# Moving the scratch writes of turned blocks from SyncE's queue to GpSimd's, and reading two kinds of them back one unit later

## The chip, the core and the metric

The kernel runs on one core of one Trainium2 chip. The metric is the device time of one execution in microseconds. The kernel before took 1476.31 us (median of 3 runs, 1476.15 to 1476.97). The execution that the profiler recorded took 1478.79 us, of which 1477.1 us lie between the first and the last instruction (the span); all stretches and waits below are of that execution.

## What is computed

One layer of a hybrid decoder for 256 tokens of width 2048, in float32, with its weights read once from HBM:

```
h = x + hybrid_mixer(rmsnorm(x))          # in-projection, SSD heads and gated short convolutions, out-projection
h = h + memory_cross_attention(rmsnorm(h), rmsnorm(mem))
h = h + (silu(h2 @ w_gate) * (h2 @ w_up)) @ w_down      # h2 = rmsnorm(h)
return rmsnorm(h)

# hybrid_mixer
proj = h @ w_in                            # 2048 -> 11296 columns
z, xbc, dt, sc_u, sc_b, sc_c = split(proj)
xbc = silu(causal_conv(xbc));  y = ssd(xs, dt, a, B, C) + xs * d_skip
y_ssd = grouped_rmsnorm(y * silu(z));  y_sc = grouped_rmsnorm(sc_b * causal_conv(sc_c * sc_u))
return concat(y_ssd, y_sc) @ w_out
```

## The kernel before

**Weights.** All weight matrices stream through the core in one fixed order (`stream_plan`, L138), as tiles of 128x1024 float32 (512 KB), each loaded by one DMA of SyncE's queue (L214) into one of six buffers `r`. Each tile is split in two: ScalarE rounds it to `h` (L254) and VectorE takes the rest, `l = r - h` (L255); the buffer of `r` is free when VectorE is done with it. TensorE multiplies in fp32r: activation parts times `h` (L328, L329) and times `l` (L332), 12 matmuls of 128x512 for a tile, into PSUM tiles `a` of 128 tokens by 512 columns.

**Units.** The program is written out unit by unit (`unit`, L401). A unit holds two weight tiles as a rule (one in the value, output and first gate tiles); it issues loads up to six tiles ahead, splits its tiles and the next two, emits the matmuls, and after the first part of the unit advances every running follow-up by one step. The follow-ups (`group_post`, `u_post`, `to_features`, `heads` and those that they call) are generators: a `yield` puts what follows it into the next unit. TensorE and SyncE run their instructions in exactly this order; on ScalarE, VectorE and GpSimd a scheduler sets the order at build time.

**Pair units.** Some units take a pair of tiles with 21 matmuls in place of 24 (`seven_mm`, L647: L657, L658, L660). They need sums of the two tiles first (`pair_sums`, L223): four VectorE additions (L229 to L232), three ScalarE roundings (L236) and three VectorE subtractions (L237), besides the split of both tiles. The sums take a buffer `b`, of which there are two.

**Turned blocks.** The result of a column group has tokens on the partitions, and what comes next needs features there. So the result is scaled (L359), transposed in 32x32 blocks by VectorE into a buffer `b` (`turn_blocks`, L343, L347), written to a scratch `w` in DRAM (`put`, L362, the DMA of L365, 512 KB) and read back rearranged into a buffer `f` (`get`, L368, the DMA of L372, 512 KB). This is done 42 times: for 22 column groups of the in-projection (`group_post`, L595), 11 gate blocks of the FFN (`u_post`, L304), 7 blocks of the residual (`to_features`, L1002; an eighth goes by TensorE) and for keys and queries (`heads`, L1133). In `group_post` and `u_post` the write is issued one unit after the transposition, the read-back one unit after the write, and the work on `f` one unit after that. All 42 writes and all 42 reads are issued by SyncE, in the same queue as the weight loads. What reads `f` first is, on the in-projection's groups, the copy of a convolution (L740), a silu (L848), or a product (L872, L889); in the FFN it is the split of the gate block (L1319, L1320).

**GpSimd** has little to do before: the setup, a reciprocal square root at a time (L308, L903, L1400) and, once for each of the four SSD groups, six `affine_select` masks (L714, L718 in `decay`, L696) on tiles that a DMA of ScalarE's queue has brought (`s<-acsT`).

Of the kernel before, what the change touches and what calls it, by code (L numbers as in the profile page):

```python
# [150 lines left out]
def trunk(tc, wst, vecs, xp, xtp, mp, mtp, wdt_in, nfin, outp):  # L151
    nc = tc.nc
# [8 lines left out]
    with ExitStack() as ctx:  # L161
# [18 lines left out]
        def nm(s):  # L180
            cnt[0] += 1
            return f"{s}{cnt[0]}"

        def slot(shape=(128, 512), dt=F32):
            return sp.tile(list(shape), dt, tag="s", name=nm("s"))
# [157 lines left out]
        def turn_blocks(src):  # L343

            t = bp.tile([128, 1024], F32, tag="b", name=nm("b"))
            for tb in range(2):
                nc.vector.transpose(t[:, tb * 512:tb * 512 + 512], src[tb])  # L347
            return t

        def scaled(accs, r, adds=None):  # L350

            o = [slot() for _ in range(2)]
            for tb in range(2):
                src = accs[tb]
                if adds is not None:
                    c, op = adds[tb]
                    tt(o[tb], src, c, op)
                    src = o[tb]
                act(o[tb], src, AF.Identity, scale=r[:, tb:tb + 1])  # L359
            return o  # L360

        def put(t):  # L362

            w = drp.tile([2, 128, 512], F32, tag="w", name=nm("w"), bufs=2)
            nc.sync.dma_start(w.rearrange("t p k -> p t k"), t.rearrange("p (t k) -> p t k", t=2))  # L365
            return w

        def get(w):  # L368


            d = fp.tile([128, 1024], F32, tag="f", name=nm("f"))
            nc.sync.dma_start(d.rearrange("p (x c) -> p x c", x=8),  # L372
                              w.rearrange("t (a i) (b c) -> (i b) (t a) c", a=4, b=4))
            return d.rearrange("p (x f j) -> p f x j", x=8, f=4)
# [220 lines left out]
        def group_post(n, accs):  # L595
            t = turn_blocks(scaled(accs, scales["x"], in_corr.pop(n, None)))
            yield
            w = put(t)
            yield
            d = get(w)  # L600
            yield
            if isinstance(groups[n], tuple):
                yield from posts[groups[n][0]](groups[n][1], d)
                return
            for f, (kind, _, j) in enumerate(groups[n]):
                p = posts[kind](j, d[:, f])
                if next(p, 0) is None:
                    procs.append(p)
                if f < 3 and not (kind == "xs" and j % 2 == 0):
                    yield  # L610
# [52 lines left out]
        def first_unit(kt):  # L663

            def part(key, o, ps):
                tok_mm(ps, key, side_blocks(xn, kt - o), (0, 1), kt == 0, kt == KT - 1, (o,))

            def loads():
                if kt + 2 < KT:
                    prep_x(kt + 2)  # L670

            if kt == 0:
                unit([([("a0",)], lambda: (part(("a0",), 0, first[0]), loads())),
                      ([("b0",)], lambda: part(("b0",), 0, first[1]))])
            else:
                key = ("ab", kt)
                unit([([key], lambda: (part(key, 0, first[0]), part(key, 1, first[1]), loads()))],
                     [group_post(0, first[0]), after(2, group_post(1, first[1]))] if kt == KT - 1 else None)
# [269 lines left out]
        for parts in in_units():  # L948
            keys = [k for part in parts for k in part]
            for _, n, c in keys:  # L950
                if n not in iaccs:
                    iaccs[n] = [acc(), acc()]
                    if len(parts[0]) == 2 and n % 2:
                        shared["in", n - 1] = [msc() for _ in range(4)]
                if c == 1:
                    for one in [] if isinstance(groups[n], tuple) else groups[n]:
                        if one[0] == "B" and one[2] > 0:
                            procs.append(decay(one[2]))
            _, n, c = keys[-1]
            quiet = len(parts[0]) == 2  # L960
            post = [group_post(k[1], iaccs[k[1]]) for k in keys if k[2] == KT // 2 - 1]
            unit([(list(part), lambda part=part: in_mm(part)) for part in parts], None, not quiet)
            for q in post:
                next(q)
                procs.append(q)
            if len(parts[0]) == 2:
                in_post(n - 1, shared["in", n - 1])
# [30 lines left out]
        def wait(k):  # L998
            for _ in range(k):
                yield  # L1000
# [132 lines left out]
        def heads(accs, r, dst, steps=(1, 1, 1)):  # L1133

            t = turn_blocks(scaled(accs, r))
            yield from wait(steps[0])
            w = put(t)
            yield from wait(steps[1])
            d = get(w)
            yield from wait(steps[2])  # L1140
            with tc.high_priority():
                for i in range(2):
                    a = slot()
                    o = a.rearrange("p (f x j) -> p f x j", f=2, x=8)
                    if i:
                        nc.vector.tensor_copy(o, d[:, 2:4])
                    else:
                        nc.scalar.copy(o, d[:, 0:2])
                    dst.append(a)

        KTs, Vs, qs = [], [], []
        for m, tiles in (("k", mh), ("q", h1g)):
            accs = [acc(), acc()]
            last = KT // 2 - 2
            for c in range(0, last, 2):
                unit([([(m, k)], lambda k=k: tok_mm(accs, (m, k), side_blocks(tiles, 2 * k), (0, 1), k == 0, False))
                      for k in (c, c + 1)])

            def last_mm(tb):
                for k in (last, last + 1):  # L1160
                    tok_mm(accs, (m, k), side_blocks(tiles, 2 * k), (tb,), False, k == last + 1)

            keys = [(m, last), (m, last + 1)]
            unit([(keys, lambda: last_mm(0)), (keys, lambda: last_mm(1))],
                 heads(accs, scales["mem"], KTs) if m == "k" else heads(accs, xa["sc"], qs, (2, 1, 0)))
# [121 lines left out]
        def whole(m, n, tb, ps):  # L1287

            if n not in SEVEN:
                return ps  # L1290
            c, op = corr[n][m, tb]
            tt(c, ps, c, op)  # L1292
            return c
# [10 lines left out]
        def u_post(n, accs):  # L1304
            while n not in gate:
                yield
            for tb in range(2):
                s = gate[n][tb]
                stt(s, whole("u", n, tb, accs[tb]), ff["r"][:, tb:tb + 1], s, ALU.mult, ALU.mult)  # L1309
            t = turn_blocks(gate[n])  # L1310
            yield
            w = put(t)
            yield
            d = get(w)
            yield
            for i in range(2):
                hi, lo = slot(dt=F32R), slot(dt=F32R)
                hv, lv = [a.rearrange("p (f x j) -> p f x j", f=2, x=8) for a in (hi, lo)]
                nc.scalar.copy(hv, d[:, 2 * i:2 * i + 2])  # L1319
                tt(lv, d[:, 2 * i:2 * i + 2], hv.bitcast(F32), ALU.subtract)  # L1320
                gs[2 * n + i] = hi, lo
# [15 lines left out]
        for i, parts in enumerate(ffn_units()):  # L1337
            if i == len(ffn_units()) - 3:
                token_sums(("d", 0, 0), [gs[0]])
            if i == 8:  # L1340
                for c in range(3):
                    token_sums(c, [(h2g[2 * c + k][:, 0:T], h2g[2 * c + k][:, T:]) for k in range(2)], c == 2)
            post = []
            for part in parts:
                m, n, c = part[0]
                for k in part:
                    if k[2] == 0:
                        faccs[k[:2]] = [acc(), acc()]
                if len(part) == 2:
                    if c == 0:  # L1350
                        shared[n] = [msc() for _ in range(4)]
                    elif c == SEVEN[n] - 1:
                        post.append(p_post(n, shared[n]))
                elif c == KT // 2 - 1:
                    post.append((g_post if m == "g" else u_post)(n, faccs[m, n]))
            unit([(list(part), lambda part=part: part_mm(part)) for part in parts], post or None)
# [274 lines left out]
```

## Time and profile before

| quantity | value |
|---|---|
| median of 3 runs | 1476.31 us |
| the profiled execution | 1478.79 us |
| its span | 1477.1 us |
| TensorE busy in the span | 1461.6 us (99%) |
| VectorE, ScalarE, GpSimd busy | 1279.7, 885.4, 38.5 us |
| mean granted TensorE clock | 0.999 |
| bytes moved by DMA | 350.91 MB, 238 GB/s in the mean |

The stages of the span: the first 16 tiles to about 50 us, the rest of the in-projection to about 600 us, out-projection and attention to about 770 us, the FFN's gate and up projections to about 1240 us, its down projection to 1468 us. In the views, a row of the timeline gives start and length in us, engine, line, operation, output <- input, and in brackets the idle time before it and what ended it. SPq is SyncE's DMA queue; its waits hold up what stands behind them in that queue. In the views of before, line numbers are those of the code above; the changed code has one more from L600 on and two more from L1314 on.

### The profile page before, as it was taken

The page shows a single profiled execution, that of the slowest core. Times are in us where ns is not written, and L with a number is a line of the kernel's source. Part 1 is how long each engine was busy: PE and PEld are TensorE (multiplying, and loading weights), DVE is VectorE, ACT ScalarE, POOL GpSimd, SP SyncE. Part 2 cuts the span into 40 slices and gives each one's busy share as a digit, 9 for nine tenths or more (in the row PEclk, how much of TensorE's full clock was granted, in tenths as well). Part 3 has the DMA queues.
Part 4 walks back from the last instruction along what each step waited for, and adds up shares of the span by engine and source line. Part 5 has one row for each costly group of instructions (what it writes and reads, how often), then busy time and mean ns, then how long its engine had stood idle before and what let it go on. Part 6 is the DMA issues. An engine that isn't in the chain of part 4 may idle for free.

```text
span 1477.1 us, 18980 instructions
## 1 busy us (share of the span) xinstructions
PE 1461.6 (99%) x6568; PEld 1203.6 (81%) x6568; DVE 1279.7 (87%) x1865; ACT 885.4 (60%) x1263; POOL 38.5 (3%) x46
## 2 busy tenths in 40 slices
PE   9999999999999999999999999999999999999997
PEld 7778888888887888888888888888888887888886
DVE  6678899989999775897578999999999998979995
ACT  7576665967765544665466665556655554655663
POOL 0012000101000000000000000000000000000000
PEclk9999999999999999999999999999999999999999
DMA  9777758769677575777648766656676667765553
GB/s 362 248 251 263 259 202 296 253 215 313 224 258 261 193 262 188 253 270 279 224 171 295 265 220 224 220 215 225 228 247 247 220 228 229 268 228 190 195 201 112
DMA packets 151520, 350.91 MB, mean 238 GB/s; under 512 B 11616, under 2 KB 63232, under 8 KB 151424
## 3 DMA queue, kind: packets, MB, share of 16 engines
q1 hardware_dynamic: 142368, 342.83, 66.1%
q10 hardware_dynamic: 9056, 6.87, 1.6%
q8 instruction: 51, 0.84, 0.2%
q14 instruction: 45, 0.37, 0.1%
HBM read 323.40 MB, written 26.26 MB: 237 GB/s over the span
## 4 chain that ended last, share of the span: by engine, by line
PE 67%; DVE 1%; issue 0%; ACT 0%; DVEq 0%; POOLq 0%; POOL 0%
PE a L328 17%; PE a L329 17%; PE a L332 17%; PE m L660 3%; PE m L657 3%; PE m L658 3%; PE a L658 2%; PE a L657 2%; PE a L660 2%; PE m L1207 0%; PE m L1176 0%; PE m L804 0%; PE m L1195 0%; DVE g L1309 0%; DVE f L1292 0%
## 5 line engine op out<-in xcount | busy, mean ns | idle before, releaser
L254 ACT CAST h<-r 128x1024 fp32r<-128x1024 f32 (+1 forms) x539 | 562.3, 1047 | 401.7 <-PE a L329 190.0
L255 DVE TENSOR_TENSOR l<-r,h 128x1024 fp32r<-128x1024 f32 (+1 forms) x539 | 649.5, 1216 | 120.3 <-ACT h L254 114.9
L328 PE MATMUL a<-h,s 128*128 128x512 f32 x1671 | 655.0, 392 | 1.1 <-ACT h L254 1.1
L329 PE MATMUL a<-h,s 128*128 128x512 f32 x1671 | 651.0, 390 | 0.0
L332 PE MATMUL a<-l,s 128*128 128x512 f32 x1671 | 450.0, 390 | 0.0
L328 PEld LDWEIGHTS a<-h,s 128*128 128x128 f32 x1671 | 313.9, 188 | 68.2 <-ACT h L254 2.2
L332 PEld LDWEIGHTS a<-l,s 128*128 128x128 f32 x1671 | 313.7, 188 | 65.6 <-DVE l L255 0.4
L329 PEld LDWEIGHTS a<-h,s 128*128 128x128 f32 x1671 | 314.1, 188 | 64.0
L236 ACT CAST s<-b 128x512 fp32r<-128x512 f32 x110 | 67.6, 618 | 71.3 <-DVE b L229 65.4
L237 DVE TENSOR_TENSOR s<-b,s 128x512 fp32r<-128x512 f32 x110 | 75.6, 687 | 0.8 <-ACT s L236 0.7
L347 DVE STREAM_TRANSPOSE b<-s 128x512 f32<-128x512 f32 x62 | 40.9, 691 | 7.2 <-ACT s L359 7.2
L229 DVE TENSOR_TENSOR b<-r,r 128x512 f32<-128x512 f32 x55 | 37.7, 686 | 10.3 <-DMA r<-in_w_dram 9.8
L230 DVE TENSOR_TENSOR r<-r 128x512 f32<-128x512 f32 x55 | 37.9, 689 | 0.8
L232 DVE TENSOR_TENSOR r<-b,r 128x512 f32<-128x512 f32 x55 | 37.7, 686 | 0.1
L237 DVE TENSOR_TENSOR s<-r,s 128x512 fp32r<-128x512 f32 x55 | 37.7, 685 | 0.0
L236 ACT CAST s<-r 128x512 fp32r<-128x512 f32 x55 | 33.9, 617 | 6.2 <-DVE r L232 5.1
L231 DVE TENSOR_TENSOR b<-b,r 128x512 f32<-128x512 f32 x55 | 37.7, 685 | 0.0
L745 DVE SCALAR_TENSOR_TENSOR t<-t,vec,t 128x255 f32<-128x255 f32 (+2 forms) x72 | 32.4, 479 | 2.8 <-ACT t L742 2.3
L657 PE MATMUL m<-s,t 128*128 128x512 f32 x76 | 29.6, 389 | 0.0
L660 PE MATMUL m<-s,t 128*128 128x512 f32 x76 | 29.6, 389 | 0.0
L658 PE MATMUL m<-s,t 128*128 128x512 f32 x76 | 29.6, 389 | 0.0
L660 PE MATMUL m<-l,s 128*128 128x512 f32 x72 | 28.1, 391 | 1.2 <-DVE l L255 1.2
(248 smaller groups left out, 1395.4 us busy)
## 6 DMA issues: line engine op xcount, KB each, us to landing
r<-in_w_dram SPq DMA_DIRECT2D x535, 512.0 KB, 4.8
w<-b SPq DMA_DIRECT2D x42, 512.0 KB, 3.3
f<-w SPq DMA_DIRECT2D x42, 512.0 KB, 4.8
s<-acsT ACTq DMA_DIRECT2D x24, 256.0 KB, 5.5
s<-in_xt_dram SPq DMA_DIRECT2D x16, 256.0 KB, 6.9
s<-in_mt_dram SPq DMA_DIRECT2D x8, 256.0 KB, 5.2
s<-in_m_dram SPq DMA_DIRECT2D x8, 256.0 KB, 5.8
parked<-s SPq DMA_DIRECT2D x8, 256.0 KB, 8.1
```

The costliest lines, as they stand in the source:

```text
L230: tt(u[:, a], u[:, a], u[:, b], ALU.add)
L236: nc.scalar.copy(h, x)
L237: tt(l, x, h.bitcast(F32), ALU.subtract)
L254: nc.scalar.copy(h[:, c], r[:, c])
L255: tt(l[:, c], r[:, c], h[:, c].bitcast(F32), ALU.subtract)
L328: mm(ps[tb], ah, h[:, w], start=first and i == ks[0], stop=False)
L329: mm(ps[tb], al, h[:, w], start=False, stop=False)
L332: mm(ps[tb], blocks(i, tb)[0], l[:, i * 512:i * 512 + 512], start=False, stop=stop and i == ks[-1])
L347: nc.vector.transpose(t[:, tb * 512:tb * 512 + 512], src[tb])
L657: mm(ps, ah, bh, start=any(ps is q for q in start), stop=False)
L658: mm(ps, al, bh, start=False, stop=False)
L660: mm(ps, ah, bl, start=False, stop=any(ps is q for q in stop))
```

## The change

`put` takes the queue that issues its DMA, GpSimd's unless another is given. `heads` gives SyncE's, so its two writes stay where they were; the other 40 writes move. All 42 reads stay on SyncE. `group_post` and `u_post` get a second `yield` between write and read-back, so that in 33 cases the read, and what the program emits behind it, come one unit later.

```diff
-        def put(t):
+        def put(t, queue=nc.gpsimd):
 
             w = drp.tile([2, 128, 512], F32, tag="w", name=nm("w"), bufs=2)
-            nc.sync.dma_start(w.rearrange("t p k -> p t k"), t.rearrange("p (t k) -> p t k", t=2))
+            queue.dma_start(w.rearrange("t p k -> p t k"), t.rearrange("p (t k) -> p t k", t=2))
             return w
...
         def group_post(n, accs):
             t = turn_blocks(scaled(accs, scales["x"], in_corr.pop(n, None)))
             yield
             w = put(t)
+            yield
             yield
             d = get(w)
             yield
...
         def heads(accs, r, dst, steps=(1, 1, 1)):
             t = turn_blocks(scaled(accs, r))
             yield from wait(steps[0])
-            w = put(t)
+            w = put(t, nc.sync)
...
         def u_post(n, accs):
...
             t = turn_blocks(gate[n])
             yield
             w = put(t)
+            yield
             yield
             d = get(w)
             yield
```

How the order moves is shown at three places. The first is SyncE's queue around the second and the third column group (numbers 1 and 2, counted from 0). Before, with `w_780` and `f_827` of group 1, `w_829` and `f_871` of group 2:

```order
L365 DMA w_780<-b_699 128x2x512
L214 DMA r_802<-in_w_dram 128x1024
L214 DMA r_813<-in_w_dram 128x1024
L372 DMA f_827<-w_780 128x8x128
L365 DMA w_829<-b_808 128x2x512
L214 DMA r_851<-in_w_dram 128x1024
L214 DMA r_853<-in_w_dram 128x1024
L372 DMA f_871<-w_829 128x8x128
L214 DMA r_893<-in_w_dram 128x1024
L214 DMA r_895<-in_w_dram 128x1024
```

After, where `f_865` is the read-back of group 1 and `f_911` that of group 2:

```order
L214 DMA r_802<-in_w_dram 128x1024
L214 DMA r_813<-in_w_dram 128x1024
L214 DMA r_849<-in_w_dram 128x1024
L214 DMA r_851<-in_w_dram 128x1024
L372 DMA f_865<-w_780 128x8x128
L214 DMA r_887<-in_w_dram 128x1024
L214 DMA r_889<-in_w_dram 128x1024
L372 DMA f_911<-w_827 128x8x128
L214 DMA r_933<-in_w_dram 128x1024
L214 DMA r_935<-in_w_dram 128x1024
```

The writes are gone from the queue. The read-back of group 2 stands behind six of these loads in place of four, and none of the six stands behind a write.

The same groups on GpSimd. Before, its queue holds only the masks of the first SSD group there:

```order
L308 TENSOR_TENSOR rr_516<-rv_514,half 128x2
L714 AFFINE_SELECT s_750<-s_750 128x2x128
L718 AFFINE_SELECT s_752<-s_752 128x512
L714 AFFINE_SELECT s_754<-s_754 128x2x128
L714 AFFINE_SELECT s_756<-s_756 128x2x128
L718 AFFINE_SELECT s_758<-s_758 128x512
L714 AFFINE_SELECT s_760<-s_760 128x2x128
```

After, `w_827` is the write of group 2, and `w_655` and `w_780` are those of groups 0 and 1:

```order
L365 DMA w_655<-b_616 128x2x512
L365 DMA w_780<-b_697 128x2x512
L715 AFFINE_SELECT s_748<-s_748 128x2x128
L719 AFFINE_SELECT s_750<-s_750 128x512
L715 AFFINE_SELECT s_752<-s_752 128x2x128
L715 AFFINE_SELECT s_754<-s_754 128x2x128
L719 AFFINE_SELECT s_756<-s_756 128x512
L715 AFFINE_SELECT s_758<-s_758 128x2x128
L365 DMA w_827<-b_808 128x2x512
```

The write of group 2 stands behind all six masks.

The second place is ScalarE's order ahead of the first pair unit (its tiles are `r_893` and `r_895` before, `r_887` and `r_889` after; the first of its sums is rounded by the first L236). Before:

```order
L740 COPY t_920<-f_871 128x256
L729 ACTIVATE s_758<-s_758,nacs 128x128
L742 ACTIVATE t_922<-t_920,vec 128x256
L740 COPY t_970<-f_871 128x256
L742 ACTIVATE t_972<-t_970,vec 128x256
L254 CAST h_978<-r_893 128x1024
L746 ACT_TABLE_LOAD
L746 ACTIVATE s_919<-t_922 128x256
L746 ACTIVATE s_919<-t_972 128x256
L236 CAST s_987<-b_982 128x512
L254 CAST h_999<-r_895 128x1024
```

After, from the instruction that reads `f_911` first to the one ahead of that L236 (just ahead of them all stands the L254 of `r_887`):

```order
L741 COPY t_960<-f_911 128x256
L730 ACTIVATE s_756<-s_756,nacs 128x128
L743 ACTIVATE t_962<-t_960,vec 128x256
L728 ACTIVATE s_754<-s_754,nacs 128x256
L254 CAST h_989<-r_889 128x1024
L730 ACTIVATE s_756<-s_756,nacs 128x128
L741 COPY t_1084<-f_911 128x256
L728 ACTIVATE s_758<-s_758,nacs 128x256
L743 ACTIVATE t_1086<-t_1084,vec 128x256
L730 ACTIVATE s_756<-s_756,nacs 128x128
L747 ACT_TABLE_LOAD
L747 ACTIVATE s_959<-t_962 128x256
```

The first reader of `f` still stands ahead of the pair's roundings; the second cast of the pair moved ahead of them, and four exponentials of the decay (L728, L730) moved in.

The third place is VectorE's order at the pair unit near 461 us. Before, ahead of its sums (L229 on) stand products and splits of a norm (L836, L275):

```order
L502 COPY memr<-rr_4511 128x2
L836 SCALAR_TENSOR_TENSOR t_4516<-s_3390,vec,m_4468 128x256
L836 SCALAR_TENSOR_TENSOR t_4521<-s_3399,vec,m_4468 128x256
L255 TENSOR_TENSOR l_4527<-r_4451,h_4526 128x1024
L275 TENSOR_TENSOR s_4518<-t_4516,s_4518 128x256
L275 TENSOR_TENSOR s_4523<-t_4521,s_4523 128x256
L229 TENSOR_TENSOR b_4530<-r_4451,r_4453 128x512
```

After:

```order
L502 COPY memr<-rr_4506 128x2
L255 TENSOR_TENSOR l_4517<-r_4431,h_4516 128x1024
L229 TENSOR_TENSOR b_4520<-r_4431,r_4433 128x512
L230 TENSOR_TENSOR r_4433<-r_4433 128x512
L231 TENSOR_TENSOR b_4520<-b_4520,r_4433 128x512
L237 TENSOR_TENSOR s_4526<-b_4520,s_4525 128x512
```

The norm's four instructions no longer stand ahead of the sums; they come behind them.

## The prediction

> **What bounds the kernel now.** I read the page first, then TensorE's waits, then those of SyncE's queue and of ScalarE, and last the timeline at the few places where TensorE stood still.
>
> ```profile
> PE 1461.6 (99%) x6568; PEld 1203.6 (81%) x6568; DVE 1279.7 (87%) x1865; ACT 885.4 (60%) x1263; POOL 38.5 (3%) x46
> ...
> PE m L660 <- DVE l L255: 2.1, 2, 1.2
> PE m L468 <- POOL U L464: 1.8, 1, 1.8
> PE a L328 <- ACT h L254: 1.1, 1, 1.1
> PE m L657 <- ACT s L926: 1.1, 1, 1.1
> PE m L657 <- ACT h L254: 1.0, 1, 1.0
> ```
>
> TensorE is busy for 1461.6 of 1477.1 us and waits for another engine 7.1 us in all, in six waits. Two of these (1.8 and 1.1) lie at the start, before any block is turned. So the change can give at most 4.2 us: 1.0 and 1.2 at the first pair unit near 100 us, 1.1 at the pair unit near 464 us, 0.9 at the one near 1245 us.
>
> The queue that the change relieves does stand still for long:
>
> ```profile
> SPq L365 <- DVE b L347: 162.0, 28, 15.0
> SPq L372 <- DMA w<-b: 66.6, 39, 3.8
> ...
> ACT h L254 <- DMA r<-in_w_dram: 21.9, 15, 3.6
> ```
>
> SyncE waits at a write for VectorE's transposition (162.0 us over 28 writes, once 15.0) and at a read-back for the landing (66.6 us), with the weight loads behind. Of all this ScalarE feels 21.9 us as weights that come late, and TensorE only what is in the four waits above. About 0.2% (3 us) is what a measurement of this kernel can tell from no change, so the whole prize is barely over that.
>
> **Whether those waits come from the writes.** The first pair unit:
>
> ```profile
> 66.30 0.38 SPq L372 DMA_DIRECT2D f<-w  x1
> 81.83 0.38 SPq L365 DMA_DIRECT2D w<-b  x1
> ...
> 85.79 0.38 SPq L372 DMA_DIRECT2D f<-w  x1
> ...
> 89.23 1.05 ACT L254 CAST h<-r 128x1024 fp32r<-128x1024 f32 x1 [2.15 <-DMA r<-in_w_dram]
> ...
> 92.70 0.41 ACT L740 COPY t<-f 128x256 f32<-128x256 f32 x1 [0.37 <-DMA f<-w]
> ...
> 94.74 1.03 ACT L254 CAST h<-r 128x1024 fp32r<-128x1024 f32 x1
> 95.79 1.28 ACT L746 ACT_TABLE_LOAD   x1
> ...
> 98.31 0.62 ACT L236 CAST s<-b 128x512 fp32r<-128x512 f32 x1
> 99.08 1.04 ACT L254 CAST h<-r 128x1024 fp32r<-128x1024 f32 x1
> ...
> 97.69 0.39 PE L657 MATMUL m<-h,s 128*128 128x512 f32 x1
> 97.92 0.39 PE L658 MATMUL m<-h,s 128*128 128x512 f32 x1
> ...
> 100.17 0.50 PE L657 MATMUL m<-h,s 128*128 128x512 f32 x1 [0.96 <-ACT h L254]
> ...
> 102.60 0.50 PE L660 MATMUL m<-l,s 128*128 128x512 f32 x1 [1.23 <-DVE l L255]
> ```
>
> From 66.7 to 81.8 us SyncE stands at the write of group 2; no load goes out. So ScalarE waits 2.15 us for weights at 89.2, runs late through 92.7 to 99.1, and its second cast of the pair (99.08) and what VectorE makes of it come 0.96 and 1.23 us late: yes, this is the write's doing.
>
> Near 464 us a late load is part of it, but so is VectorE's order:
>
> ```profile
> 452.60 1.06 ACT L254 CAST h<-r 128x1024 fp32r<-128x1024 f32 x1 [1.65 <-DMA r<-in_w_dram]
> ...
> 453.88 0.87 DVE L836 SCALAR_TENSOR_TENSOR t<-s,vec,m 128x256 f32<-128x256 f32 x2
> ...
> 455.80 0.76 DVE L275 TENSOR_TENSOR s<-t,s 128x256 fp32r<-128x256 f32 x2
> 456.47 0.69 DVE L229 TENSOR_TENSOR b<-r,r 128x512 f32<-128x512 f32 x1
> ...
> 465.06 0.50 PE L657 MATMUL m<-s,s 128*128 128x512 f32 x1 [1.08 <-ACT s L926]
> ```
>
> The pair's sums begin (456.47) behind the norm's products and splits (0.87 + 0.76 us).
>
> Near 1245 us neither queue has a part:
>
> ```profile
> 1237.40 1.29 DVE L1292 TENSOR_TENSOR f<-a,f 128x512 f32<-128x512 f32 x2 [1.04 <-PE a L332]
> ...
> 1241.15 0.65 DVE L229 TENSOR_TENSOR b<-r,r 128x512 f32<-128x512 f32 x1
> ...
> 1246.18 0.50 PE L660 MATMUL m<-l,t 128*128 128x512 f32 x1 [0.88 <-DVE l L255]
> ```
>
> VectorE waits for TensorE's own last product of the gate block, turns it, and only then sums the next pair. This order is unchanged, so the 0.9 us stay.
>
> **The change part by part.** *The write leaves SyncE.* 40 issues and their waits go from its queue; loads go out as buffers come free. Off the path this is worth nothing; on it, only at the two places above.
>
> *The write on GpSimd.* No row of before shows a DMA issued there. Its cost is bounded by the landings of the same write from SyncE and the read-back's:
>
> ```profile
> DMA to landing us min/median/max: 2.8/3.3/8.7
> DMA to landing us min/median/max: 4.0/4.8/7.8
> 85.32 0.58 POOL L714 TENSOR_SCALAR_AFFINE_SELECT s<-s 128x256 f32<-128x256 f32 x1
> L714 POOL TENSOR_SCALAR_AFFINE_SELECT s<-s x16: 401/586/1500, 80.0 to 358.7; 128x256 f32<-128x256 f32 x16
> ```
>
> I take 3.3 us, the median, as the transfer is the same; the ends are 2.8 and 8.7. Queued behind a write on GpSimd are reciprocal roots and masks; these wait at most for a transposition that TensorE's order also waits for, and no chain of before ends in them, so nothing there. What stands *ahead* of a write matters more. The write of group 2 now stands behind six masks, of which the last runs from 85.32 to 85.90, while its block was turned by 81.8. So it is issued at 85.9, 4.1 us later than before; it lands at 89.2, and the read-back, issued then, at 89.2 + 4.8 = 94.0 in place of 92.7. SyncE stands at that read-back for some 10 us, but the loads are out (in the order above six stand ahead of it in place of four, none behind a write), enough for the pair.
>
> *First pair unit, worked out.* The pair's casts no longer wait for loads, but ScalarE's order still has the first reader of `f` ahead of the sums' roundings. From 92.70 to 98.31 ScalarE took 5.6 us from that reader to the first L236, 0.3 of it waiting. The new order has four exponentials more (0.35 us each by start to start) and one silu less (0.6): 5.3 + 1.4 - 0.6 = 6.1 us. So the first rounding starts at 94.0 + 6.1 = 100.1 and ends at 100.7. TensorE wants it after eight matmuls of 0.227 us from 97.69, at 99.5: it waits 1.2. The second rounding stands one cast behind (1.0 + 0.6 = 1.6 us later) and is wanted four matmuls (0.9) later: 0.7 more. The third, again 1.6 later, is wanted two matmuls (0.5) later: 1.1 more. Sum 3.0 us in place of 2.2: **+0.8**. With a write of 2.8 us it is +0.3, with 8.7 us +6.2, since the wait grows one for one; no wait at all would be -2.2.
>
> [...]
>
> *Pair unit near 464 us.* Four instructions (1.6 us) move from ahead of the sums to behind them, and the load is no longer late. The wait of 1.1 us is covered: **-1.1**.
>
> *The extra unit.* It moves the read-back behind two more loads (SyncE issues no second wait for it) and the emission of its followers one unit, 24 matmuls or 5.4 us, later. In the FFN:
>
> ```profile
> 832.70 0.61 ACT L1319 CAST s<-f 128x512 fp32r<-128x512 f32 x1
> ...
> 834.63 0.69 DVE L1320 TENSOR_TENSOR s<-f,s 128x512 fp32r<-128x512 f32 x1
> ...
> DMA to landing us min/median/max: 3.0/3.0/3.5
> ...
> 820.00:1240.00 420.00, 420.00 (x1855) 347.91 (x1854) 398.32 (x516) 241.61 (x299) 0.00 (x0) 1.00 0.66 230
> ```
>
> ScalarE's and VectorE's orders have these splits after as many weight splits as before. VectorE comes to its part 1.3 us after ScalarE has done the other (833.3 to 834.6), so a landing 1.3 us later costs nothing, and VectorE has 420 - 398.3 = 21.7 us to spare over ten blocks, 2.2 each. Zero, unless the write takes over 3.0 + 1.3 + 2.2 = 6.5 us. The last gate blocks are used over ten tiles later, the last column groups over twenty, so neither end waits.
>
> **Sum.** 1478.8 + 0.8 - 1.1 = 1478.5 for a profiled execution, whose time is 2.5 us over the median of the runs; on the median, 1476.3 - 0.3 = **1476.0 us**.
>
> **The rivals.** (1) *Both waits go*: the masks run earlier, or the scheduler's order leaves enough slack. -2.2 - 1.1 = -3.3, 1473.0 us, just faster. For it: the loads' delay is really gone. Against: the masks wait for DMAs of ScalarE's queue, which now meet weight loads on the way.
> (2) *The write of group 2 comes too late* (the other side): it stands behind the masks, so ScalarE stands at `f` ahead of the first pair's roundings, and each us of the write beyond 3.3 costs TensorE one. Slower by 3 us from a write of 3.3 + 3.3 = 6.6 us on; with 8.7, 1476.3 + 6.2 - 1.1 = 1481.4. Middle 1480.3.
> (3) *Writes from GpSimd are slow everywhere*: over 6.5 us each, VectorE's spare time in the FFN is used up, ten times. At 8.7 us: 10 x 2.2 = 22 us more, about 1503.
> (4) *Nothing changes*: only the issue was ever saved, 1476.3 us; the waits of ScalarE move from loads to `f`. [...]
>
> **How the numbers follow.** Forecast 0.60, (1) 0.13, (2) 0.12, (3) 0.05, (4) 0.10. Forecast and (4) lie within 0.2%: 0.70; faster 0.13; slower 0.17. The range runs from 1472.5, half a us below (1) (three runs of the same kernel lie 0.8 us apart), to the middle of (2), 1480.3; outside lie (3) and half of (2), 0.11.
>
> **What would show it.** Right: no SyncE wait at L365 but for the two of `heads`; the write of group 2 issued just behind the sixth mask near 86 us; TensorE's waits near 100 us of 2 to 4 us, none near 464, 0.9 near 1245; ScalarE's wait for weights well under 21.9 us. Wrong: no wait near 100 us (then 1), writes that land after over 6 us (then 2 or 3), or new waits of TensorE at other pair units, for which I have no term.

## The result, and the profile after

The changed kernel takes 1488.39 us (median of 4 runs, 1484.57 to 1489.25), the kernel before beside it 1476.64. The ratio, which goes by all runs and not by the two medians, is 1.0074, with a 95% interval of 1.0059 to 1.0089: slower by 0.74%. Between the medians lie 11.8 us, where no change was forecast (1476.0, 1472.5 to 1480.3). The profiled execution took 1488.43 us, with a span of 1486.7 us, 9.6 us more than before.

TensorE's work is the same, 6568 matmuls. Its waits come first, then those of SyncE's queue and of ScalarE:

```profile
PE m L658 <- ACT s L236: 2.7, 1, 2.7
PE m L658 <- DVE t L837: 2.0, 1, 2.0
PE m L468 <- POOL U L464: 1.8, 1, 1.8
PE m L658 <- ACT s L927: 1.8, 1, 1.8
PE a L658 <- DVE s L357: 1.3, 1, 1.3
PE m L661 <- DVE l L255: 0.9, 1, 0.9
PE a L658 <- ACT s L359: 0.8, 1, 0.8
```

```profile
SPq L372 <- DMA w<-b: 101.0, 34, 13.3
...
SPq L365 <- DVE b L347: 15.1, 2, 8.9
...
ACT t L741 <- DMA f<-w: 10.4, 3, 4.7
...
ACT h L254 <- DMA r<-in_w_dram: 2.6, 4, 0.8
```

The change does what it says. SyncE waits at a write only for the two of `heads` (15.1 us in place of 162.0), and weights hardly come late any more (ScalarE waits 2.6 us in place of 21.9). In exchange SyncE stands longer at the read-backs (101.0 in place of 66.6 us), and the readers of `f` wait, in `ACT t L741` alone 10.4 us. TensorE's waits grow from 7.1 to 11.7 us in all, with three at pair units where there were none (near 241, 288 and 380 us).

That is only half of the 9.6 us. The rest shows in two stretches of the table by windows, here after and before for the same windows (behind the window stand its length, the busy time of TensorE, its weight loads, VectorE, ScalarE and GpSimd, each with its number of instructions, then the granted clock, the share of DMA and GB/s):

```profile
96.00:106.00 10.00, 6.70 (x21) 4.03 (x20) 9.12 (x14) 9.98 (x18) 0.00 (x0) 0.83 0.61 230
376.00:387.00 11.00, 9.09 (x33) 6.72 (x32) 9.59 (x14) 9.25 (x20) 0.73 (x1) 0.84 0.92 337
```

```profile
96.00:106.00 10.00, 7.81 (x34) 5.79 (x33) 9.97 (x15) 9.46 (x14) 0.00 (x0) 1.00 0.41 154
376.00:387.00 11.00, 11.00 (x59) 8.64 (x58) 10.82 (x22) 4.82 (x8) 0.00 (x0) 1.00 0.95 322
```

In 376 to 387 us TensorE starts 33 matmuls where it started 59, at a granted clock of 0.84 and not 1.00; part of the difference is that 16 shorter matmuls (L804, L806) fall into the window before. The timeline of the changed kernel around the stall of the first pair unit, with a granted clock of 1.00 from 98.0 to 101.5 us and of 0.50 from 101.9 to 105.3 us:

```profile
98.54 0.39 PE L659 MATMUL m<-h,s 128*128 128x512 f32 x1
101.61 0.55 PE L658 MATMUL m<-s,s 128*128 128x512 f32 x1 [2.68 <-ACT s L236]
101.95 0.63 PE L659 MATMUL m<-s,s 128*128 128x512 f32 x1
102.38 0.63 PE L661 MATMUL m<-l,s 128*128 128x512 f32 x1
102.81 0.63 PE L661 MATMUL m<-s,s 128*128 128x512 f32 x1
```

Behind the stall (98.54 to 101.61) the matmuls start 0.43 us apart (101.95, 102.38, 102.81), not 0.227. So I measure by starts: every distance of over 0.3 us between two starts, less the usual 0.227, summed over a place.

| place, us | before | after |
|---|---|---|
| first pair unit, 98 to 106 | 2.7 | 5.9 |
| pair unit near 241 | - | 2.3 |
| pair unit near 288 | - | 1.9 |
| pair unit near 380 | - | 3.9 |
| pair unit near 464 (474 after) | 1.3 | - |
| pair unit near 1245 (1255 after) | 1.2 | 1.2 |
| sum | 5.2 | 15.2 |

The growth of 10.0 us accounts for the span's 9.6. In 14 to 600 us 15 matmuls start 0.38 to 0.6 us apart, which makes 3.4 us of it; before there is none there.

### The profile page after: what moved, and what is told of

It is laid out like the page before. It is cut to its first block, busy times and chain, and to the rows that moved or that the text cites. A ratio compares the mean times of both kernels' runs of the same rounds, so it can differ in the third digit from the quotient of the medians.

```text
span 1486.7 us, 19011 instructions
## 1 busy us (share of the span) xinstructions
PE 1466.3 (99%) x6568; PEld 1204.6 (81%) x6568; DVE 1281.5 (86%) x1865; ACT 885.2 (60%) x1265; POOL 64.6 (4%) x86
## 4 chain that ended last, share of the span: by engine, by line
PE 91%; issue 3%; DVE 2%; DMA 2%; ACT 1%; POOL 0%; DVEq 0%; POOLq 0%; ACTq 0%; SPq 0%
PE a L328 24%; PE a L329 24%; PE a L332 24%; PE m L661 3%; PE m L658 3%; PE m L659 3%; PE a L658 2%; PE a L659 2%; PE a L661 2%; DMA s<-acsT 1%; DMA r<-in_w_dram 1%; ACT h L254 1%; PE m L328 0%; PE m L332 0%; PE m L329 0%
## 5 line engine op out<-in xcount | busy, mean ns | idle before, releaser
L254 ACT CAST h<-r 128x1024 fp32r<-128x1024 f32 (+1 forms) x539 | 561.0, 1046 | 366.4 <-PE a L329 171.5
L328 PE MATMUL a<-h,s 128*128 128x512 f32 x1671 | 654.6, 392 | 0.3 <-ACT h L254 0.3
L329 PE MATMUL a<-h,s 128*128 128x512 f32 x1671 | 650.8, 389 | 0.0
L236 ACT CAST s<-b 128x512 fp32r<-128x512 f32 x110 | 67.8, 617 | 66.2 <-DVE b L229 59.1
L365 POOL DMA_DIRECT2D w<-b x40 | 29.5, 738 | 951.4 <-DVE b L347 706.5
L229 DVE TENSOR_TENSOR b<-r,r 128x512 f32<-128x512 f32 x55 | 37.9, 690 | 7.9 <-DMA r<-in_w_dram 7.8
L236 ACT CAST s<-r 128x512 fp32r<-128x512 f32 x55 | 33.9, 617 | 9.6 <-DVE r L232 8.4
L359 ACT ACTIVATE s<-s,xr 128x512 f32<-128x512 f32 x32 | 22.0, 717 | 16.3 <-DVE s L357 10.7
L658 PE MATMUL a<-h,s 128*128 128x512 f32 x72 | 28.5, 395 | 2.0 <-DVE s L357 1.3
L661 PE MATMUL m<-s,t 128*128 128x512 f32 x76 | 29.6, 389 | 0.0
```

The lines of the kernel that those rows point to most:

```text
L236: nc.scalar.copy(h, x)
L254: nc.scalar.copy(h[:, c], r[:, c])
L328: mm(ps[tb], ah, h[:, w], start=first and i == ks[0], stop=False)
L329: mm(ps[tb], al, h[:, w], start=False, stop=False)
L658: mm(ps, ah, bh, start=any(ps is q for q in start), stop=False)
L661: mm(ps, ah, bl, start=False, stop=any(ps is q for q in stop))
```

## The experiments

All runs keep the computation. Line numbers shift by one or two with the edits: L657, L658 and L659 are the same matmul, L926 to L928 the same copy, L791 to L794 the same product. "Late" means that the work on `f` is written out one unit later. Each ratio is against the kernel before on the same chip, by all runs of both, with its 95% interval; differences in us in the text are between medians. Losses by starts are those of the one profiled execution.

| run | what differs | us | ratio |
|---|---|---|---|
| e1 | queue alone | 1491.0 | 1.0100 (1.0086 to 1.0114) |
| e2 | extra unit alone | 1490.3 | 1.0092 (1.0078 to 1.0106) |
| e3 | changed, column groups undone | 1477.3 | 1.0004 (0.9995 to 1.0013) |
| e4 | changed, mask writes by SyncE | 1488.3 | 1.0086 (1.0072 to 1.0100) |
| e5 | before, all groups late | 1486.3 | 1.0058 (1.0045 to 1.0071) |
| e6 | changed, groups another unit late | 1485.7 | 1.0069 (1.0056 to 1.0081) |
| e7 | queue alone, mask writes by SyncE | 1479.6 | 1.0024 (1.0014 to 1.0033) |
| e8 | before, even groups 4 to 12 late | 1477.0 | 1.0000 (0.9992 to 1.0009) |
| e9 | before, odd groups late | 1491.8 | 1.0100 (1.0084 to 1.0117) |
| e10 | before, mask writes by GpSimd | 1490.5 | 1.0094 (1.0081 to 1.0107) |
| e11 | before, all groups two units late | 1480.0 | 1.0022 (1.0013 to 1.0031) |
| e12 | as e13, mask writes by SyncE | 1477.1 | 1.0006 (0.9997 to 1.0015) |
| e13 | changed, extra unit only in even groups 4 to 12 and the FFN | 1486.3 | 1.0067 (1.0055 to 1.0080) |
| e14 | before, one mask write by GpSimd | 1482.3 | 1.0035 (1.0022 to 1.0049) |
| e15 | as e14, ScalarE's order held | 1482.3 | 1.0039 (1.0026 to 1.0051) |
| e16 | control of e15 | 1480.4 | 1.0025 (1.0015 to 1.0035) |
| e17 | as e9, PSUM tiles freed early | 1482.0 | 1.0035 (1.0022 to 1.0047) |
| e18 | as e4, PSUM tiles freed early | 1484.6 | 1.0056 (1.0043 to 1.0068) |

### Which half of the change

The edits: e1 has `queue=nc.gpsimd` in `put` and no extra `yield` (the residual's seven writes are back with SyncE in this run); e2 has the extra `yield`s and `queue=nc.sync`; e3 is the changed kernel with

```diff
-            w = put(t)
+            w = put(t, nc.sync)
             yield
-            yield
             d = get(w)
```

in `group_post`.

> The writes move to GpSimd's queue, the read-backs stay one unit after the write as before. Theory D (the extra unit is what costs: read-backs stand two loads further back and the followers' readers of f stand in ScalarE's and VectorE's order ahead of the pair sums): within 3 us of before, 1474 to 1479 us, TensorE's waits 5 to 9 us in all. Theory Q (writes issued by GpSimd come later, behind its masks, and so the read-backs): as slow as the changed kernel or slower, 1486 to 1495 us, since the read-back now reaches the head of SyncE's queue earlier and holds up the loads behind it. Theory B (both together are needed): under 4 us slower than before.

> All writes stay in SyncE's queue, the read-backs come one unit later. Theory D: as slow as the changed kernel, 1484 to 1491 us, with the same stalls of TensorE near 100, 240, 289 and 379 us. Theory Q: as before, 1474 to 1479 us, without those stalls. Theory B: under 4 us slower than before.

> The column groups of the in-projection are as before (write by SyncE, read-back one unit later than it); the FFN's gate blocks and the residual's blocks keep the change. All theories that put the loss in the in-projection: 1475 to 1478 us, no new wait of TensorE. If the FFN's writes by GpSimd cost something: 1480 us or more, with TensorE waiting behind L1321 between 820 and 1250 us.

Each half alone costs as much as both (1.0100 and 1.0092 against 1.0074), which none of the three theories had foreseen: the costs don't add. And all of it lies in the 22 column groups; writes by GpSimd in the FFN and the residual, and the extra unit in the FFN, cost nothing (e3, 1.0004).

### The queue's half: four writes behind masks

The writes of groups 2, 4, 10 and 14 stand behind the masks of the SSD groups on GpSimd. In the changed kernel, first GpSimd, then SyncE and ScalarE around group 2:

```profile
82.16 0.41 POOL L715 TENSOR_SCALAR_AFFINE_SELECT s<-s 128x256 f32<-128x256 f32 x1 [28.32 <-DMA s<-acsT]
...
87.30 0.45 POOL L715 TENSOR_SCALAR_AFFINE_SELECT s<-s 128x256 f32<-128x256 f32 x1
87.70 0.73 POOL L365 DMA_DIRECT2D w<-b  x1
```

```profile
90.94 0.38 SPq L372 DMA_DIRECT2D f<-w  x1
...
95.00 0.41 ACT L741 COPY t<-f 128x256 f32<-128x256 f32 x1 [4.65 <-DMA f<-w]
...
100.95 0.60 ACT L236 CAST s<-b 128x512 fp32r<-128x512 f32 x1
```

The masks wait for their tiles and end at 87.75; the write goes at 87.70, the read-back at 90.94, `f` is read at 95.00 after a wait of 4.65 us, and the first rounding of the pair starts 6.0 us behind that. In the changed kernel the writes of groups 2, 4 and 14 start as their last mask ends; that of group 10 waits last for its own block (0.4 us behind the masks). e4 and e7 issue these four writes from SyncE (`put(t, nc.sync if n in (2, 4, 10, 14) else nc.gpsimd)`), in the changed kernel and with the queue alone; e10 is the kernel before with only these four on GpSimd.

> The changed kernel, but the writes of column groups 2, 4, 10 and 14, which stood behind the masks on GpSimd, are issued by SyncE again (three of them waited 4.5, 5.5 and 5.9 us there behind masks). Theory M (the masks ahead of these writes make f late): TensorE's stalls near 98 and 379 us go, the others stay; 1481 to 1484 us. Theory O (the order of ScalarE's and VectorE's work one unit later is what costs): 1486 to 1491 us, as the changed kernel.

> Writes by GpSimd but for column groups 2, 4, 10 and 14 (SyncE), and no extra unit anywhere; beside it, the run of the queue alone took 1491.0. Theory M: 1476 to 1484 us, the long stall near 99 us (3.8 us there) and the one near 371 us (2.7 us) gone. Theory L (a read-back that stands on SyncE for a write issued elsewhere holds up the loads, masks or not): 1487 to 1493 us.

> The kernel before with four writes alone moved to GpSimd: column groups 2, 4, 10 and 14, which stand behind masks there. Moving all but these cost 3.2 us, moving these too 14.4 us. Theory M (the masks ahead make the cost, and costs add): 1485 to 1490 us. Theory I (the four cost only together with the others, since every moved write meets weight loads on the way): 1477 to 1481 us.

Of the 14.4 us that the queue alone costs, 11.4 go with these four (1491.0 to 1479.6; e7 also has the residual's seven writes on GpSimd, where they cost nothing in e3), and the four alone make 13.7 (e10): the theory of the masks holds in the kernel before, and the other 36 writes cost 3 us (e7). But inside the changed kernel their removal gains nothing (e4), so something else is enough there too.

How do the masks cost? e14 moves the write of group 2 alone. In e15 and its control e16, priority is given to the exponentials of the first SSD group (`with tc.high_priority()` for `g == 0` around the two `act(t, t, AF.Exp, ...)` of `decay`), so that ScalarE's and VectorE's orders are the same in both, whoever issues the write.

> The kernel before with one write alone moved to GpSimd, that of group 2, behind the six masks of the first SSD group; the four such writes together cost 13.7 us. Theory M (each costs at its own pair unit): the stall near 98 us with its slow matmuls (6.6 us there, 2.7 in the kernel before) stays, those near 200 and 370 us go; 1479 to 1483 us.

> As the kernel with the write of group 2 alone on GpSimd, but the exponentials of the first SSD group have priority when ScalarE's order is set; with that, ScalarE's and VectorE's orders are those of its control (the same priority, the write with SyncE) instruction for instruction, and only the queue of one write differs. Theory L (the write behind the masks lands late, and that alone costs): 3 to 6 us more than the control. Theory B (what costs is the order that ScalarE gets at build time when the write stands behind the masks, with two more table loads on the pair's path): within 1.5 us of the control.

> The control: the kernel before, with priority for the exponentials of the first SSD group when ScalarE's order is set; all writes with SyncE. Both theories: 1474 to 1479 us.

One write costs 5.3 us between the medians; of 4.3 us in the span, 3.8 lie at the first pair unit by starts. ScalarE there in e14, and what TensorE has of it:

```profile
93.09 0.41 ACT L740 COPY t<-f 128x256 f32<-128x256 f32 x1 [3.06 <-DMA f<-w]
...
96.17 1.28 ACT L746 ACT_TABLE_LOAD   x1
97.46 0.42 ACT L746 ACTIVATE s<-t 128x256 f32<-128x256 f32 x1
97.89 1.28 ACT L729 ACT_TABLE_LOAD   x1
99.18 0.40 ACT L729 ACTIVATE s<-s,nacs 128x128 f32<-128x128 f32 x1
99.59 1.28 ACT L746 ACT_TABLE_LOAD   x1
...
101.20 0.60 ACT L236 CAST s<-b 128x512 fp32r<-128x512 f32 x1
...
102.81 0.80 PE L657 MATMUL m<-h,s 128*128 128x512 f32 x1 [3.50 <-ACT h L254]
```

`f` comes only 0.4 us later than before (93.09, was 92.70), yet the first rounding starts 2.9 us later (101.20, was 98.31): the order set at build time changed with the queue of the write, and an exponential came to stand between two silus, with two more table loads of 1.28 us. With the order held the write costs 1.9 us between the medians (1482.3 and 1480.4); that is outside both bands I had written down, and the intervals overlap. The control missed its band too: it is 3.5 us slower than the kernel before, with a stall of its own near 90 us, behind early exponentials that wait 2.07 us for a mask. The first reader of `f` in e15, then in e16:

```profile
96.20 0.40 ACT L741 COPY t<-f 128x256 f32<-128x256 f32 x1 [2.57 <-DMA f<-w]
```

```profile
94.78 0.41 ACT L741 COPY t<-f 128x256 f32<-128x256 f32 x1 [0.63 <-DMA f<-w]
```

With `f` read 1.4 us later, and ScalarE's and VectorE's orders the same, e15 loses 6.3 us by starts at the first pair unit (103 to 112 us), e16 0.4; near 90 us e15 loses 2.6 and e16 4.0. So a late `f` alone is enough for a stall of this size there, though the executions differ by less in all, and that of e15 is the slowest of its five. What the changed order adds in e14 stays open.

Near group 14 the masks cost in another way. In e10 the place near 370 us loses 4.1 us by starts, and not in a pair unit:

```profile
366.09 0.69 DVE L229 TENSOR_TENSOR b<-r,r 128x512 f32<-128x512 f32 x1 [6.54 <-DMA r<-in_w_dram]
...
369.67 1.66 PE L332 MATMUL a<-l,s 128*128 128x512 f32 x4 [2.49 <-DVE l L255]
```

VectorE stands at the first sum of the next pair, whose load is not there, and the split `l` that a plain unit needs comes behind it. The kernel before has no wait at this sum.

### The extra unit's half: the odd groups

e5 is the kernel before with one more `yield` behind `d = get(w)` in `group_post`: SyncE's queue is then the same to the last instruction. e6 has it in the changed kernel, e11 twice in the kernel before; e8 has it under `if n % 2 == 0 and 2 < n < 14`, e9 under `if n % 2`.

> The kernel before; SyncE's queue is untouched to the last instruction (all writes and reads as before), and only the work on f of the column groups is written out one unit later than before. Theory O (the work on f collides with the pair units when it comes one unit later): 1484 to 1491 us, TensorE stalls of 2 us and more in the in-projection, and no engine waiting for f at them. Theory R (the read-backs that stand two loads further back, and so land later, cost): 1475 to 1478 us.

> The changed kernel with the work on f of the column groups another unit later. Theory F (the changed kernel's stalls come from f that lands later than its readers' place in ScalarE's and VectorE's order): a unit is 5.4 us, more than the longest wait for f (4.9 us), so those waits and the stalls near 98 and 241 us go; 1476 to 1482 us. Theory O: nothing gained, 1486 to 1495 us, with stalls at other pair units.

> The kernel before, SyncE's queue untouched, the work on f one unit later for the even column groups 4 to 12 alone (the short convolutions' parts; for every group it cost 8 to 10 us). Theory P (the late unit costs where an even group's work meets the pair unit, which its readers of f already touch in the kernel before: sums at 227.6, 270.3, 362.8 us, readers at 229.4, 272.5, 365.2): 1480 to 1487 us. Theory S (it costs in the state chain of the SSD groups, the odd ones, which ends in the products L792 and the copies L927 that TensorE waited for): 1475 to 1478 us.

> The kernel before, SyncE's queue untouched, the work on f one unit later for the odd column groups alone. Theory S: 1482 to 1488 us, as if all groups were late, with TensorE waiting for L792 or L927 at the pair units near 236, 371 and 419 us. Theory P: 1475 to 1478 us.

> The kernel before, SyncE's queue untouched, the work on f of all column groups two units later; one unit cost 8 to 10 us. If only the meeting with the pair unit costs, two units pass it by: 1475 to 1480 us. If any shift of this work costs, because the order before fits as it is: 1483 to 1492 us.

No landing is needed: the later work alone costs (e5: 1.0058, which is 8.6 us; 10.0 between the medians). In e6 the waits for `f` near 98 and 241 us did go as theory F said, but 6.2 us came up at 280 to 291 us; late data is not what holds the sum up. It is the odd groups (15.0 us, e9), which from 3 to 19 carry the SSD heads; five even ones are free (e8, 1.0000). The odd groups alone cost more than all groups together (10.0, e5), and more than the band I had written down; no run shows why. Two units are cheaper than one (3.1 us, e11), so the cost does not grow with the shift: it seems to be a matter of what the work meets. What it meets shows near 370 us, TensorE and VectorE, before and after:

```profile
361.75 0.60 PE L788 MATMUL m<-ident,s 128*128 128x128 f32 x4
362.17 0.76 DVE L791 TENSOR_TENSOR s<-m,dtn 128x256 f32<-128x256 f32 x2 [1.44 <-PE m L788]
...
370.40 0.39 PE L657 MATMUL m<-h,s 128*128 128x512 f32 x1
```

```profile
373.85 0.60 PE L789 MATMUL m<-ident,s 128*128 128x128 f32 x4
377.06 0.39 PE L658 MATMUL m<-h,s 128*128 128x512 f32 x1
...
380.82 0.50 PE L658 MATMUL m<-s,s 128*128 128x512 f32 x1 [1.79 <-ACT s L927]
...
381.66 0.72 DVE L792 TENSOR_TENSOR s<-m,dtn 128x256 f32<-128x256 f32 x2
```

A late SSD group transposes its `xs` into two of the four PSUM tiles `m` (373.85) just ahead of the pair unit, which wants four (377.06). Before, that was 8.7 us ahead of it, and VectorE had emptied both tiles at 362.9. Now VectorE does the pair's sums, splits and two transpositions first and empties them at 381.66. TensorE gets on when the pair's own first product is copied out (L927). e17 gives VectorE's product that empties them priority, in the kernel of e9; e18 does so in the changed kernel, with the four writes by SyncE:

```diff
-            tt(xd, pt[...]..., dtn[...]..., ALU.mult)
+            with tc.high_priority():
+                tt(xd, pt[...]..., dtn[...]..., ALU.mult)
```

> The kernel before with the odd groups' work one unit later (1491.8 us), and priority for the product L794 when VectorE's order is set: it reads the transposed blocks out of two of the four PSUM tiles m. Near 371 us it then stands 6 places behind the first pair sum in place of 17, and near 428 us 4 in place of 16. Theory P (the pair unit's products find their PSUM tiles still held by the transposed blocks of the late SSD groups): the waits for L793 and L928 at these two units go, 1478 to 1485 us. If the plain amount of work on VectorE and ScalarE there is the cause: 1488 to 1494 us.

> The changed kernel with all its extra units kept, both causes mended in another way than by undoing: the four writes behind masks with SyncE, and the same priority for the product that frees the PSUM tiles. Without the priority it took 1488.3 us. Theory P: 1477 to 1483 us. If the late unit costs by other ways too: 1485 to 1490 us.

e9, then e17, at the same pair unit:

```profile
370.86 0.60 PE L790 MATMUL m<-ident,s 128*128 128x128 f32 x4
...
378.82 0.50 PE L659 MATMUL m<-s,s 128*128 128x512 f32 x1 [2.78 <-ACT s L928]
...
380.90 0.74 DVE L793 TENSOR_TENSOR s<-m,dtn 128x256 f32<-128x256 f32 x2
381.46 0.77 PE L659 MATMUL m<-s,s 128*128 128x512 f32 x1 [1.44 <-DVE s L793]
```

```profile
371.75 0.60 PE L790 MATMUL m<-ident,s 128*128 128x128 f32 x4
...
373.13 0.75 DVE L794 TENSOR_TENSOR s<-m,dtn 128x256 f32<-128x256 f32 x2
...
379.20 0.50 PE L659 MATMUL a<-h,s 128*128 128x512 f32 x1 [0.46 <-DVE s L357]
```

With the tiles emptied 7.8 us earlier both waits are gone (and those near 428 us), and 9.8 of the 15.0 us with them. So held PSUM tiles are the larger part in this kernel, as far as the priority acts through them alone: some other instructions of VectorE and ScalarE changed places with it. Of what is left, most lies at the first pair unit (6.2 us by starts, 98 to 109 us, where the kernel before loses 2.7), 1.4 near 243 and 0.7 near 379 us. In the changed kernel the priority gains only 3.7 us (e18, 1488.3 to 1484.6, between the two bands I had written down). In e18 0.9 us are left near 378 us, where the changed kernel loses 3.9 near 380; 4.2 at the first pair unit and 1.7 near 286 us stay. So there the late unit costs in other ways as well, which I did not take apart.

### Both together

e12 is the changed kernel with the four writes by SyncE and the extra unit kept only for the even groups 4 to 12 (`if n % 2 == 0 and 2 < n < 14`) and in the FFN (so it is gone from the even groups 0, 2 and 14 to 20 too, which no run moved by themselves); e13 has only the second of these.

> The changed kernel without its two suspected parts: the writes of groups 2, 4, 10 and 14 (those behind masks) stay with SyncE, and the extra unit between write and read-back is kept only for the even groups 4 to 12 and in the FFN. Theory M+S (the masks ahead of four writes, and the odd groups' late unit, are the whole loss): 1475 to 1480 us. If something else in the change costs as well: 1483 us or more.

> The changed kernel with the extra unit kept only for the even groups 4 to 12 and in the FFN; the four writes still stand behind masks on GpSimd. It is the last corner of a square: both causes 1488.4 (the changed kernel), only the late odd groups 1488.3, neither 1477.1. If the masks alone are enough for the loss: 1486 to 1492 us. If they need the late unit of the odd groups: 1477 to 1481 us.

TensorE's waits in e12, all of them:

```profile
PE m L662 <- DVE l L255: 2.0, 2, 1.1
PE m L468 <- POOL U L464: 1.8, 1, 1.8
PE a L328 <- ACT h L254: 0.3, 1, 0.3
PE a L659 <- DVE s L357: 0.3, 1, 0.3
```

Without both the time of before is back (1.0006), with either it is not (1.0067, 1.0086), and with both it is no worse (1.0074). One reason that they don't add is the first pair unit, where either is enough: by starts e4 loses 7.2 us there (in an execution 5.0 us over its median), e13 7.6, and the changed kernel with both 5.9. The second losses are not at one place. e4 and the changed kernel lose 4.0 and 3.9 us at the pair unit near 380; e13 loses 3.0 near 368, in a plain unit where TensorE waits 2.6 us for `l`, as e10 does near 370. Why the changed kernel does not lose that too is not shown. No run beat the kernel before.

## Why the prediction was wrong

*Where the gain could be.* Right: the prize was at most a few us. The wait near 464 us is gone as forecast (-1.1), the 0.9 us near 1245 us stayed.

*The write on GpSimd.* Nearly right: forecast to land in 3.3 us between 2.8 and 8.7. Write, then read-back, in the changed kernel:

```profile
DMA to landing us min/median/max: 3.0/3.9/8.0
DMA to landing us min/median/max: 3.9/4.6/9.1
```

The median is 0.6 us over the forecast, and the ten writes of the FFN landed in 3.9 to 4.0 us, where rival (3) needed over 6.5: it falls.

*The first pair unit.* Right in its mechanism up to the first rounding, too small in size: the write at 87.7 (forecast 85.9, as the masks ended later), landed 90.9 (89.2), `f` 95.0 (94.0), from the reader to the first rounding 6.0 us (6.1). That the waits came to 3.7 us (3.0) is in part luck: the three roundings made 2.7, 0.2 and nothing (forecast 1.2, 0.7 and 1.1), as TensorE also came to the place 0.7 us earlier (96.95, was 97.69), and 0.8 is a wait for L359, for which I had no term. And I counted waits and not starts. By starts the place lost 3.2 us more than before, not 0.8, as TensorE was slow behind the stall (0.43 us between starts). Of the rivals, (2) was nearest, and its range ended short of the result.

*The extra unit, the step that failed.* "It moves the read-back behind two more loads [...] and the emission of its followers one unit, 24 matmuls or 5.4 us, later. In the FFN: [...] Zero". For the FFN that was right (e3). For the column groups I followed only the read-back and the first reader of `f` at one place, and put the later work at nothing without a row for it. By itself it costs 8.6 us (e5; 10.0 between the medians). In the changed kernel three pair units for which the sum had no term lose 8.1 of the 10.0 us by starts (2.3, 1.9 and 3.9). One way is shown: the transposes of an SSD group, one unit later, hold two PSUM tiles into the pair unit, as near 380 us (e9 and e17). What holds up the places near 241 and 288 us, and what the late unit does at the first pair unit, stays open. The prediction did name the sign, "new waits of TensorE at other pair units, for which I have no term", and that is what came.

*Masks ahead of other writes.* I costed group 2. Groups 4, 10 and 14 have masks of their own SSD groups ahead of them, though group 10's write hardly waits for these; the three others together make 8.3 of the 13.7 us (e10 less e14).

## What to carry to other kernels

Where every engine's order fits a tight unit, a step that is moved must be followed to its last instruction and to every buffer that it holds there, PSUM tiles too, and not only to its first reader. Before a DMA moves to a "free" queue, list what computes on that engine ahead of it, at each place; and where a scheduler sets the order at build time, read the new order for what stands between (a table load, a reader ahead of a cast). Count a stall by the starts of the matmuls behind it, not by its wait (at the first pair unit 5.9 us and 3.7).

## What the runs showed of the hardware

The matmuls of 128x512 start 0.227 us apart. Behind some stalls they started about 0.427 us apart: in the changed kernel at a granted clock of 0.50 from 101.9 to 105.3 us and of 0.53 from 382.0 to 385.4 us. Eight distances from 381.62 us on, of 0.39 to 0.58 us, made 1.9 us there on top of the stall; in e9 twelve from 381.46 us on, of 0.42 to 0.57 us, made 2.5 us. In the changed kernel a distance of 2.18 us between two starts (from 378.64 us) was followed by such a stretch within a us, one of 2.41 us (from 240.75 us) was not. So the length of a stall alone did not tell whether the slow stretch came; what decided it is not shown.

ScalarE's table load took 1.28 us each time, 14 times in the kernel before and 16 times in the changed one. In the changed kernel the instruction that issues a write took 0.73 us on GpSimd (median of 40) and 0.38 us on SyncE (both of `heads`).
